# Layer-0 attention of a two-layer decoder trunk: the carry moved from DVE to ACT, third tiles for weights and probabilities, and a new instruction order

## The chip, the cores and the metric

The kernel runs on one core of a Trainium2 chip. The metric is the device time of one execution in microseconds (us), the median over runs. Work on the core goes to TensorE (PE, whose weight loads are listed apart as PEld), VectorE (DVE), ScalarE (ACT), GpSimd (POOL) and SyncE (SP), which here issues nearly all transfers.

## What is computed

A residual stream of 2048 tokens, with 16 meta tokens and padding ahead, goes through two layers and a final norm. The change lies in layer 0, an "even" layer with two attentions side by side, eight heads each: stick-breaking and a causal softmax (MLA).

```python
z = jnp.einsum('bthd,bshd->bhts', q, k) * scale          # stick-breaking
log_beta = jax.nn.log_sigmoid(z)
log_1m = jnp.where(mask, log_beta - z, 0.0)
suffix = lax.cumsum(log_1m, axis=3, reverse=True) - log_1m
a = jnp.where(mask, jnp.exp(log_beta + suffix), 0.0)
o_sb = jnp.einsum('bhts,bshd->bthd', a, v)
...
s = jnp.einsum('bthd,bshd->bhts', q, k) * scale          # causal softmax
p = jax.nn.softmax(jnp.where(mask, s, NEG), axis=-1)
o_mla = jnp.einsum('bhts,bshd->bthd', p, v)
...
h = h + jnp.concatenate([o_sb * silu(g_sb), o_mla * silu(g_mla)], -1) @ w_out
```

## The kernel before

Projections of layer 0 come first, then its attention (725 to 1624 us of the profiled execution), then its output projection and layer 1. Only the attention's order and three of its operations are touched.

The sequence is cut into 17 blocks of 122 keys. Heads are taken in 4 pairs (one head per half of the 128 output partitions), the queries in 5 groups g = 4, 3, 2, 1, 0 (four blocks of 122, so up to 488 columns; group 0 has one block). Within a pair and group, one step treats one key block of the stick-breaking part (from the diagonal back) and one of the softmax part (from the first key on). There are 17 + 13 + 9 + 5 + 1 = 45 steps a pair, 180 in all. Next to the diagonal a step is narrower: 366, 244 or 122 columns.

Each step, for both heads m = 0, 1 of the pair, consists of the operations below; the names are those of the planner, with the profile's line of before.

- stick-breaking: qks, two matmuls of scores into a PSUM tile zp (L1023, L1024); z, the mask at the diagonal on DVE (L1031); e, a softplus on ACT into sp (L1035); c, the carry: row 0 of the previous step's zp, scaled, goes to row 0 of this step's sp, on DVE (L1042); h, sp rounded to fp32r on DVE (L1050) or ACT (L1048); lo, sp minus h into l, on POOL or DVE (both L1055); tri, two matmuls of h and l with a triangular matrix, added to zp (L1060, L1061), which give the suffix sums and the next carry; a, a softplus on ACT of zp into the weights a (L1065); avs, the weights times the values into av (L1077).
- softmax: qkm, three matmuls of scores into ms (L1097 to L1099); p, on ACT into p, or acc in a group's first step (L1103); pm, the mask at the diagonal on DVE (L1109); acc, the sum of p over steps on POOL (L1115, L1117); avm, p times the values into mav (L1125).
- at a group's end: ogs and ogm (DVE, times the gates, L1087, L1131), dn, the denominators on PE (L1137), rd, their copy on ACT (L1142), rc, reciprocals on DVE (L1146), rm on POOL (L1150) and the stores.

The matmuls avs, avm and dn use 64 output columns, one head per half, so two of them stand side by side; the text calls them half-width, and a run of them between full-width matmuls a half-width run. Their inputs are f32 and show as two records for each matmul.

The order of each engine's instructions is fixed when the kernel is built. `attention_plan` lists the operations with planned costs and dependences; `list_schedule` then plays them through: an engine that is free takes, of the operations that are ready, the one of lowest rank (step number plus a constant `RANK` of its kind). `RINGS` says how many tiles there are of each kind, `MOVE` when h, lo or acc may go to another engine, `LAT` the planned delay between engines. The program emits the operations in that order, and semaphores make each wait for its inputs and tiles. An instruction that waits holds up whatever stands behind it on its engine.

Of the kernel before, what the change touches and what calls it, by code (L numbers as in the profile page):

```python
# [11 lines left out]
AF = mybir.ActivationFunctionType  # L12
ALU = mybir.AluOpType
# [113 lines left out]
def attention_plan():  # L127
# [34 lines left out]
    def gps(n):
        return n * 2.1 + 190

# [3 lines left out]
    for gi, (p, g) in enumerate(groups):  # L168
# [7 lines left out]
        tri, b_tri, acc, b_acc = ([None, None] for _ in range(4))  # L176
        prev = av = None
        for t in range(G.b1):
# [12 lines left out]
            for m in range(2):  # L191
                b_zp, b_a, b_sp, b_h, b_l = (buf(f"{x}{m}") for x in ("zp", "a", "sp", "h", "l"))
                qk_s = op("qks", s, m, "PE", pe(2, s.ns), [qk_s], [b_zp], late=late_s)
                o = qk_s
                if s.bs >= G.b0:
                    o = op("z", s, m, "DVE", 270, [o])
                o = op("e", s, m, "ACT", act(s.ns), [o], [b_sp])
                if prev:
                    o = op("c", s, m, "DVE", dve(prev.ns) + 60, [o, tri[m]], rel=[b_tri[m]])
                o = op("h", s, m, "DVE", dve(s.ns) + 200, [o], [b_h], alt=("ACT", act(s.ns)))  # L200
                o = op("lo", s, m, "Pool", gps(s.ns), [o], [b_l], [b_sp], alt=("DVE", 2.2 * dve(s.ns)))
                o = tri[m] = op("tri", s, m, "PE", pe(2, s.ns), [o], rel=[b_h, b_l])
                b_tri[m] = b_zp
                aa.append(op("a", s, m, "ACT", act(s.ns), [o], [b_a], [b_zp]))
                bz.append(b_a)
            pp, bp = [], []
            for m in range(2):
                b_ms, b_p = buf("ms"), buf(f"acc{m}" if s.first else f"p{m}")
                qk_m = op("qkm", s, m, "PE", pe(3, s.nm), [qk_m], [b_ms], late=late_m)
                x = op("p", s, m, "ACT", act(s.nm), [qk_m], [b_p], [b_ms])  # L210
                if s.bm >= G.b0:
                    x = op("pm", s, m, "DVE", 270, [x])
                pp.append(x)
                bp.append(b_p)
                if s.first:
                    acc[m], b_acc[m] = x, b_p
                else:
                    o = op("acc", s, m, "Pool", gps(s.nm), [x, acc[m]], rel=[b_p], alt=("DVE", 2.2 * dve(s.nm)))
                    acc[m] = o
                    if t == 1:  # L220
                        use(o, b_acc[m])
                        b_acc[m] = buf(f"acc{m}")
                        o.acq = [b_acc[m]]
            o = av = op("av", s, 0, "PE", pair(s.ns) + pair(s.nm) + 180, aa + pp + [av], [b_av, b_mav] if s.first else [],
                        bz + bp)
            if s.last:
# [13 lines left out]
    for o in ops:  # L240
        for d, w in o.deps:
# [9 lines left out]
HEAD = {("lo", "tri"): -200, ("a", "av"): -40, ("p", "av"): -40}
LAT = {("PE", "PE"): 0, ("PE", "ACT"): 200, ("PE", "DVE"): 200, ("PE", "Pool"): 250, ("ACT", "ACT"): 95,
       ("ACT", "PE"): 250, ("ACT", "DVE"): 200, ("ACT", "Pool"): 195, ("DVE", "DVE"): 60, ("DVE", "PE"): 320,
       ("DVE", "ACT"): 180, ("DVE", "Pool"): 230, ("Pool", "Pool"): 60, ("Pool", "PE"): 80, ("Pool", "DVE"): 80,
       ("Pool", "ACT"): 80}


def list_schedule(ops, rank=RANK, move=MOVE, rings=RINGS):
# [12 lines left out]
    busy = {e: 0 for e in engines}  # L271
    out, events, tick, now = [], [], 0, 0
    while len(out) < len(ops):
        again = True
        while again:
            again = False
            for e in engines:
                if busy[e] > now:
                    continue
                best = None  # L280
                for src in engines:
                    for o in ready[src]:
# [3 lines left out]
                        if any(len(held[b.ring]) >= rings[b.ring] and users[held[b.ring][-rings[b.ring]]] for b in o.acq):  # L286
                            continue
                        k = (pri[o][0] + (0 if own else rank["other"]), pri[o][1])
                        if best is None or k < best[0]:
                            best = (k, o, src)  # L290
                if best:
# [36 lines left out]
def build(tc, a, off, upto=99):  # L328
# [666 lines left out]
    with b2:  # L995
# [41 lines left out]
        def carry(s, m):  # L1037

            n, k = s.ns, s.prev.ns
            V.tensor_scalar(s.sp[m][0:1, n - k:n], s.prev.zp[m][0:1, :k], -1.0 / CW, None, op0=ALU.mult)  # L1042

# [19 lines left out]
        def aexp(s, m):  # L1063
            x = s.a[m] = work(f"a{m}", 2)
            S.activation(x[:BC, :s.ns], s.zp[m][:BC, :s.ns], AF.Softplus)  # L1065
# [35 lines left out]
        def pexp(s, m):  # L1101
            pt = s.pt[m] = work(f"acc{m}", 3) if s.first else work(f"p{m}", 2)
            S.activation(pt[:BK, :s.nm], s.ms[m][:BK, :s.nm], AF.Softplus, scale=MSC)  # L1103
            if s.first:
                s.G.acc[m] = pt
# [42 lines left out]
        def rmul(s, m):  # L1148
# [746 lines left out]
```

## Time and profile before

| | us |
|---|---|
| median of 3 runs | 2677.18 (2676.46 to 2677.35) |
| the profiled execution | 2672.08 |
| its span, first to last instruction | 2669.9 |
| outside the span | 2.2 |
| attention stage in it | 725 to 1624 |

| whole span | PE | PEld | DVE | ACT | POOL |
|---|---|---|---|---|---|
| busy us | 2570.5 | 1959.4 | 1587.2 | 1368.7 | 1123.5 |

The profile shows one execution. In a timeline row stand the start, the length, engine, line, operation, tiles, the number of instructions merged, and in brackets the idle time ahead of it with what the profile takes to have ended it. In a groups row stand the busy time, the mean length of one in ns and the idle time ahead. In a waits row stand the total in us, the times and the longest. A window row gives busy time and count for PE, PEld, DVE, ACT and POOL, then the granted PE clock (0.99 over the whole span), DMA share and GB/s. A wait is put down to the releaser that came last in the profile, which need not be the one that mattered.

### The profile page before, as it was taken

The page shows a single profiled execution, that of the slowest core. Times are in us where ns is not written, and L with a number is a line of the kernel's source. Part 1 is how long each engine was busy: PE and PEld are TensorE (multiplying, and loading weights), DVE is VectorE, ACT ScalarE, POOL GpSimd, SP SyncE. Part 2 cuts the span into 40 slices and gives each one's busy share as a digit, 9 for nine tenths or more (in the row PEclk, how much of TensorE's full clock was granted, in tenths as well). Part 3 has the DMA queues.
Part 4 walks back from the last instruction along what each step waited for, and adds up shares of the span by engine and source line. Part 5 has one row for each costly group of instructions (what it writes and reads, how often), then busy time and mean ns, then how long its engine had stood idle before and what let it go on. Part 6 is the DMA issues. An engine that isn't in the chain of part 4 may idle for free. (4 is left out here: it accounts for less than half of the span.)

```text
span 2669.9 us, 39152 instructions
## 1 busy us (share of the span) xinstructions
PE 2570.5 (96%) x13105; PEld 1959.4 (73%) x13105; DVE 1587.2 (59%) x3624; ACT 1368.7 (51%) x3143; POOL 1123.5 (42%) x925
## 2 busy tenths in 40 slices
PE   9999999999989999999999998999999899999998
PEld 7888889999855555555555556788999788777776
DVE  5366487777245665665575566334222567888884
ACT  6532121213255655565565553644222899986564
POOL 1012210010178878878878885300000123346551
PEclk9999999999999999999999999999999999999999
DMA  5376644342683352251230115534554345577652
GB/s 148 104 220 173 182 113 108 95 114 68 161 160 89 91 132 68 70 145 40 69 106 25 35 40 163 156 95 136 127 124 122 103 120 129 144 187 210 183 162 97
DMA packets 337860, 321.32 MB, mean 120 GB/s; under 512 B 143670, under 2 KB 319738, under 8 KB 337075
## 3 DMA queue, kind: packets, MB, share of 16 engines
q1 hardware_dynamic: 336939, 317.94, 44.6%
q8 instruction: 104, 1.70, 0.3%
q14 instruction: 97, 0.79, 0.1%
q10 hardware_dynamic: 720, 0.89, 0.1%
HBM read 198.28 MB, written 120.80 MB: 120 GB/s over the span
## 5 line engine op out<-in xcount | busy, mean ns | idle before, releaser
L1055 POOL TENSOR_TENSOR l<-sp,h 123x488 fp32r<-123x488 f32 (+2 forms) x334 | 364.3, 1095 | 109.4 <-DVE h L1050 72.0
L1597 POOL TENSOR_TENSOR s_sb<-s_sb,den 108x1008 f32<-108x1008 f32 (+1 forms) x76 | 147.4, 1940 | 548.5 <-DVE den L1596 451.9
L1117 POOL TENSOR_TENSOR acc<-acc,p 122x488 f32<-122x488 f32 (+3 forms) x288 | 329.1, 1160 | 32.0 <-ACT p L1103 17.5
L1042 DVE TENSOR_SCALAR sp<-zp 1x488 f32<-1x488 f32 (+3 forms) x320 | 183.4, 575 | 263.1 <-ACT p L1103 82.1
L406 PE MATMUL psd<-xh,wh 128*128 128x366 f32 (+1 forms) x760 | 273.8, 360 | 0.0
L408 PE MATMUL psd<-xh,wl 128*128 128x366 f32 (+1 forms) x760 | 267.3, 352 | 0.0
L407 PE MATMUL psd<-xl,wh 128*128 128x366 f32 (+1 forms) x760 | 267.2, 352 | 0.0
L1103 ACT ACTIVATE p<-ms 122x488 f32<-122x488 f32 (+3 forms) x320 | 151.9, 515 | 186.9 <-PE mav L1125 185.5
L1065 ACT ACTIVATE a<-zp 123x488 f32<-123x488 f32 (+2 forms) x360 | 175.6, 517 | 110.8 <-DVE sp L1042 80.6
L1035 ACT ACTIVATE sp<-zp 123x488 f32<-123x488 f32 (+2 forms) x360 | 180.4, 519 | 52.1 <-DVE zp L1031 26.9
L1050 DVE CAST h<-sp 123x488 fp32r<-123x488 f32 (+3 forms) x295 | 183.9, 623 | 13.2 <-ACT sp L1035 4.9
L1588 ACT ACTIVATE s_sb<-s_sb,nm 108x252 f32<-108x252 f32 (+1 forms) x304 | 149.2, 494 | 34.7 <-DVE nm L1579 34.7
L1023 PEld LDWEIGHTS zp<-q,kbig 128*123 128x123 f32 x320 | 58.8, 184 | 143.9 <-DVE h L1050 61.0
L1023 PE MATMUL zp<-q,kbig 128*123 128x488 f32 (+3 forms) x320 | 134.4, 424 | 22.9 <-ACT a L1065 19.1
L407 PEld LDWEIGHTS psd<-xl,wh 128*128 128x128 f32 x760 | 143.9, 189 | 15.8 <-issue 0.9
L406 PEld LDWEIGHTS psd<-xh,wh 128*128 128x128 f32 x760 | 143.7, 189 | 12.4 <-issue 0.7
L408 PEld LDWEIGHTS psd<-xh,wl 128*128 128x128 f32 x760 | 143.1, 188 | 10.8
L1077 PE MATMUL av<-a,vbig 123*64 123x488 f32 (+3 forms) x640 | 146.1, 535 | 2.3 <-DVE og L1087 2.3
L396 POOL TENSOR_TENSOR wl<-raw,wh 128x1024 fp32r<-128x1024 f32 x17 | 40.9, 2404 | 245.4 <-DVE wh L395 158.9
L1061 PE MATMUL zp<-l,tri_r 123*123 123x488 f32 (+2 forms) x360 | 132.2, 370 | 8.6 <-POOL l L1055 7.3
L1125 PE MATMUL mav<-p,mvbig 122*64 122x488 f32 (+3 forms) x640 | 139.0, 511 | 0.5 <-DMA mvbig<-d_mv 0.5
L1577 DVE CUSTOM_DVE_ANT_0 s_sb<-pss,bt,sinks 108x252 f32<-108x252 f32 (+1 forms) x304 | 127.3, 475 | 11.8 <-PE psg L1657 4.5
(516 smaller groups left out, 6850.0 us busy)
## 6 DMA issues: line engine op xcount, KB each, us to landing
kbig<-d_sk SPq DMA_DIRECT2D x32, 492.0 KB
q<-d_q SPq DMA_DIRECT2D x36, 432.0 KB
xt<-in_x SPq DMA_DIRECT2D x32, 448.0 KB
raw<-in_od_w_in SPq DMA_DIRECT2D x48, 256.0 KB
mq<-d_mq SPq DMA_DIRECT2D x32, 373.6 KB
raw<-in_ev_w_in SPq DMA_DIRECT2D x19, 512.0 KB
kkb<-d_kk SPq DMA_DIRECT2D x18, 472.0 KB
xt<-d_h SPq DMA_DIRECT2D x16, 512.0 KB
```

The lines of the kernel that those rows point to most:

```text
L406: T.matmul(o, wh[:, k, m0:m1], xh[:, k, c0:c1], start=(k == 0), stop=False)
L407: T.matmul(o, wh[:, k, m0:m1], xl[:, k, c0:c1], start=False, stop=False)
L408: T.matmul(o, wl[:, k, m0:m1], xh[:, k, c0:c1], start=False, stop=(k == k_n - 1))
L1023: T.matmul(zp[:BC, :s.ns], k[:, 2 * m, c], q, start=True, stop=False)
L1035: S.activation(sp[:BC, :s.ns], s.zp[m][:BC, :s.ns], AF.Softplus)
L1042: V.tensor_scalar(s.sp[m][0:1, n - k:n], s.prev.zp[m][0:1, :k], -1.0 / CW, None, op0=ALU.mult)
L1050: V.tensor_copy(h[:BC, :n], sp[:BC, :n])
L1055: on_(on).tensor_tensor(l[:BC, :n], s.sp[m][:BC, :n], f(s.h[m][:BC, :n]), op=ALU.subtract)
L1065: S.activation(x[:BC, :s.ns], s.zp[m][:BC, :s.ns], AF.Softplus)
L1103: S.activation(pt[:BK, :s.nm], s.ms[m][:BK, :s.nm], AF.Softplus, scale=MSC)
L1117: eng.tensor_tensor(g.acc[m][:BK, s.jm:g.n], g.acc[m][:BK, s.jm:g.n], s.pt[m][:BK, :n], op=ALU.add)
L1588: S.activation(s_sb[:nq, hh, :ww], s_sb[:nq, hh, :ww], AF.Exp, bias=nm[:nq, hh:hh + 1], scale=SLOPES[h], accum_out=den[:nq, hh:hh + 1])
```

## The change

The carry c becomes an ACT instruction (an activation that copies, with a scale) instead of DVE's. The rings of a and p get three tiles instead of two. In the planner, av is split into avs and avm, which can be ordered apart; its costs and delays have new numbers; a price `TURN` is put on PE going to half width, with two ranks that steer it (`few`: wait while fewer than two half-width operations are ready; `stay`: remain at half width once there). `RANK` and `MOVE` are new numbers. Everything outside the attention keeps its order; line numbers are 13 higher from qks to a and 9 higher from avs on.

```diff
     def pe(passes, n):
-        return passes * max(n / 2.24 + 6, 107)
+        return passes * max(n / 2.244 + 5, 107)
     def pair(n):
-        return 4 * (n / 2.38 + 2) + 140
+        return n / 0.6
     def dve(n):
-        return n / 0.96 + 69
+        return n / 0.96 + 75
     def act(n):
-        return n / 1.2 + 85
+        return n / 1.2 + 70
+    def two(n):
+        return n * 2.45 + 110
     def gps(n):
-        return n * 2.1 + 190
+        return n * 2.1 + 215
...
-                    o = op("c", s, m, "DVE", dve(prev.ns) + 60, [o, tri[m]], rel=[b_tri[m]])
-                o = op("h", s, m, "DVE", dve(s.ns) + 200, [o], [b_h], alt=("ACT", act(s.ns)))
-                o = op("lo", s, m, "Pool", gps(s.ns), [o], [b_l], [b_sp], alt=("DVE", 2.2 * dve(s.ns)))
+                    o = op("c", s, m, "ACT", act(prev.ns), [o, tri[m]], rel=[b_tri[m]])
+                o = op("h", s, m, "DVE", s.ns * 1.3 + 150, [o], [b_h], alt=("ACT", act(s.ns)))
+                o = op("lo", s, m, "Pool", gps(s.ns), [o], [b_l], [b_sp], alt=("DVE", two(s.ns)))
...
-            o = av = op("av", s, 0, "PE", pair(s.ns) + pair(s.nm) + 180, aa + pp + [av], [b_av, b_mav] if s.first else [],
-                        bz + bp)
+            av = op("avs", s, 0, "PE", pair(s.ns), aa + [av], [b_av] if s.first else [], bz)
+            mav = op("avm", s, 0, "PE", pair(s.nm), pp + [mav], [b_mav] if s.first else [], bp)
...
-RINGS = dict(... a0=2, a1=2, ... p0=2, p1=2, ...)
+RINGS = dict(... a0=3, a1=3, ... p0=3, p1=3, ...)
-MOVE = dict(lo=849, acc=1901, h=104)
+MOVE = dict(lo=829, acc=3122, h=0)
+HALF_WIDTH = ("avs", "avm", "dn")
+TURN = 342
...
+                if e == "PE":
+                    few = rank["few"] * (sum(o.kind in HALF_WIDTH and rt[o] <= now for o in ready[e]) < 2)
...
+                        if o.kind in HALF_WIDTH:
+                            k = (k[0] - rank["stay"] if half else k[0] + few, k[1])
...
+                    o.took = o.cost if src == e else o.alt[1]
+                    if e == "PE":
+                        o.took += TURN * (o.kind in HALF_WIDTH and not half)
+                        half = o.kind in HALF_WIDTH
...
-            V.tensor_scalar(s.sp[m][0:1, n - k:n], s.prev.zp[m][0:1, :k], -1.0 / CW, None, op0=ALU.mult)
+            S.activation(s.sp[m][0:1, n - k:n], s.prev.zp[m][0:1, :k], AF.Copy, scale=-1.0 / CW)
...
-        def values(s, _):
-            avs(s)
-            avm(s)
```

What moves is shown at one place, the full-width step 100 of the 180 (its score matmuls to its value passes: about 1220 to 1241 us in the profile of before). A row is a line, the operation, the tile written and the tiles read, and the size; digits behind a name are the head (sp0, sp1) and a tile's number.

ACT in before, from e of head 0 of step 100 on:

```order
L1035 ACTIVATE sp0_11826<-zp0_11816 123x488
L1103 ACTIVATE p0_11842<-ms_11808 122x488
L1103 ACTIVATE p1_11846<-ms_11822 122x488
L1065 ACTIVATE a0_11852<-zp0_11770 123x488
L1065 ACTIVATE a1_11858<-zp1_11793 123x488
L1035 ACTIVATE sp1_11866<-zp1_11839 123x488
```

ACT in after, from the same e on (L1048 is e, L1055 the carry, L1061 h, L1078 a, L1112 p):

```order
L1048 ACTIVATE sp0_11856<-zp0_11842 123x488
L1048 ACTIVATE sp1_11863<-zp1_11849 123x488
L1055 ACTIVATE sp0_11856<-zp0_11802 1x488
L1055 ACTIVATE sp1_11863<-zp1_11808 1x488
L1061 ACTIVATE h1_11878<-sp1_11863 123x488
L1078 ACTIVATE a0_11886<-zp0_11802 123x488
L1078 ACTIVATE a1_11888<-zp1_11808 123x488
L1112 ACTIVATE p0_11892<-ms_11858 122x488
L1112 ACTIVATE p1_11897<-ms_11868 122x488
```

A step has six ACT instructions before, and eight or nine after: both carries, and in every second step one h, stand between e and a.

DVE in before, steps 100 and 101:

```order
L1042 TENSOR_SCALAR sp0_11826<-zp0_11770 1x488
L1050 CAST h0_11860<-sp0_11826 123x488
L1042 TENSOR_SCALAR sp1_11866<-zp1_11793 1x488
L1050 CAST h1_11881<-sp1_11866 123x488
L1042 TENSOR_SCALAR sp0_11872<-zp0_11816 1x488
L1050 CAST h0_11906<-sp0_11872 123x488
L1042 TENSOR_SCALAR sp1_11912<-zp1_11839 1x488
L1050 CAST h1_11927<-sp1_11912 123x488
```

DVE in after, from step 100 on (L1063 is h, L1068 lo):

```order
L1063 CAST h0_11873<-sp0_11856 123x488
L1068 TENSOR_TENSOR l1_11882<-sp1_11863,h1_11878 123x488
L1063 CAST h0_11918<-sp0_11903 123x488
L1063 CAST h1_11926<-sp1_11907 123x488
L1063 CAST h0_11965<-sp0_11948 123x488
L1068 TENSOR_TENSOR l1_11974<-sp1_11955,h1_11970 123x488
```

The carries are gone from DVE; one h of four has gone to ACT, and one lo of four has come from POOL. Over the whole stage, lo on POOL goes from 334 to 253 and on DVE from 26 to 107; h on DVE goes from 295 to 263 and on ACT from 65 to 97. acc stays on POOL (320).

PE in before, around the half-width run that holds the value passes of step 98:

```order
L1099 MATMUL ms_11854<-mq_11253,mkbig4_10118 122x488
L1023 MATMUL zp0_11862<-q_11237,kbig0_10783 123x488
L1024 MATMUL zp0_11862<-q_11237,kbig0_10783 123x488
L1097 MATMUL ms_11868<-mq_11253,mkbig4_10118 122x488
L1098 MATMUL ms_11868<-mq_11253,mkbig4_10118 122x488
L1099 MATMUL ms_11868<-mq_11253,mkbig4_10118 122x488
L1077 MATMUL av_11527<-a0_11806,vbig0_10785 64x488
L1077 MATMUL av_11527<-a1_11812,vbig0_10785 64x488
L1125 MATMUL mav_11530<-p0_11796,mvbig0_10786 64x488
L1125 MATMUL mav_11530<-p1_11800,mvbig0_10786 64x488
L1023 MATMUL zp1_11885<-q_11237,kbig0_10783 123x488
```

PE in after, at the run that holds avs of step 96, avm of 98 and avs of 97 (L1086 is avs, L1134 avm, L1036 qks):

```order
L1106 MATMUL ms_11868<-mq_11189,mkbig4_10074 122x488
L1107 MATMUL ms_11868<-mq_11189,mkbig4_10074 122x488
L1108 MATMUL ms_11868<-mq_11189,mkbig4_10074 122x488
L1086 MATMUL av_11570<-a0_11732,vbig4_10075 64x488
L1086 MATMUL av_11570<-a1_11747,vbig4_10075 64x488
L1134 MATMUL mav_11425<-p0_11760,mvbig0_10742 64x488
L1134 MATMUL mav_11425<-p1_11764,mvbig0_10742 64x488
L1086 MATMUL av_11570<-a0_11794,vbig4_10075 64x488
L1086 MATMUL av_11570<-a1_11796,vbig4_10075 64x488
L1036 MATMUL zp0_11894<-q_11283,kbig0_10739 123x488
L1037 MATMUL zp0_11894<-q_11283,kbig0_10739 123x488
L1036 MATMUL zp1_11900<-q_11283,kbig0_10739 123x488
```

Before, each step's two value passes form one run, between the score matmuls of head 0 and head 1 of one step. After, two runs stand in two steps: one with three passes, of steps 96 to 98, as here, and one with avm alone; the score matmuls of both heads come together. Over the stage there are 187 half-width runs before and 165 after.

More of the change, by code (lines that the diff above doesn't have):

```diff
@@ L176, in attention_plan @@
         tri, b_tri, acc, b_acc = ([None, None] for _ in range(4))
-        prev = av = None
+        prev = av = mav = None
         for t in range(G.b1):
@@ L211, in attention_plan @@
                 if s.bm >= G.b0:
-                    x = op("pm", s, m, "DVE", 270, [x])
+                    x = op("pm", s, m, "DVE", 300, [x])
                 pp.append(x)
@@ L217, in attention_plan @@
                 else:
-                    o = op("acc", s, m, "Pool", gps(s.nm), [x, acc[m]], rel=[b_p], alt=("DVE", 2.2 * dve(s.nm)))
+                    o = op("acc", s, m, "Pool", gps(s.nm), [x, acc[m]], rel=[b_p], alt=("DVE", two(s.nm)))
                     acc[m] = o
@@ L246 @@
 DMA_NS = 6000
-RINGS = dict(zp0=2, zp1=2, a0=2, a1=2, sp0=2, sp1=2, h0=2, h1=2, l0=2, l1=2, av=1, mav=1, ms=2,
-             p0=2, p1=2, acc0=3, acc1=3, og=2, rd=1)
-RANK = dict(qks=-15.42, z=10.15, e=21.37, rc=-14.75, c=-16.52, h=27.44, lo=-11.85, tri=-8.67, a=-7.29, av=26.38, ogs=21.25, qkm=-2.11, p=-8.52, pm=-4.52, acc=-36.25, ogm=5.1, dn=1.09, rd=-4.23, rm=0.64, head=0.54, other=2.43)
-MOVE = dict(lo=849, acc=1901, h=104)
[L251 to L255, printed above, removed]
+RINGS = dict(zp0=2, zp1=2, a0=3, a1=3, sp0=2, sp1=2, h0=2, h1=2, l0=2, l1=2, av=1, mav=1, ms=2,
+             p0=3, p1=3, acc0=3, acc1=3, og=2, rd=1)
+RANK = dict(qks=-48.53, z=-16.4, e=36.5, rc=-42.98, c=-9.66, h=11.42, lo=-30.91, tri=-5.03, a=4.01, avs=5.07, avm=3.11, ogs=23.02, qkm=-2.2, p=-10.76, pm=2.07, acc=-41.78, ogm=12.82, dn=-0.45, rd=8.86, rm=-7.51, head=0.23, other=11.93, few=12.47, stay=8.39)
+MOVE = dict(lo=829, acc=3122, h=0)
+HEAD = {("lo", "tri"): -200, ("a", "avs"): -40, ("p", "avm"): -40}
+HALF_WIDTH = ("avs", "avm", "dn")
+TURN = 342
+LAT = {("PE", "PE"): 0, ("PE", "ACT"): 200, ("PE", "DVE"): 250, ("PE", "Pool"): 250, ("ACT", "ACT"): 45,
+       ("ACT", "PE"): 200, ("ACT", "DVE"): 80, ("ACT", "Pool"): 155, ("DVE", "DVE"): 60, ("DVE", "PE"): 160,
+       ("DVE", "ACT"): 50, ("DVE", "Pool"): 145, ("Pool", "Pool"): 0, ("Pool", "PE"): 30, ("Pool", "DVE"): 0,
+       ("Pool", "ACT"): 0}
 def list_schedule(ops, rank=RANK, move=MOVE, rings=RINGS):
@@ L271, in list_schedule @@
     busy = {e: 0 for e in engines}
-    out, events, tick, now = [], [], 0, 0
+    out, events, tick, now, half = [], [], 0, 0, False
     while len(out) < len(ops):
@@ L296, in list_schedule @@
                     o.on, o.start = e, now
-                    busy[e] = now + (o.cost if src == e else o.alt[1])
+                    o.took = o.cost if src == e else o.alt[1]
+                    if e == "PE":
+                        o.took += TURN * (o.kind in HALF_WIDTH and not half)
+                        half = o.kind in HALF_WIDTH
+                    busy[e] = now + o.took
                     tick += 1
@@ L1063, in aexp, with avs @@
         def aexp(s, m):
-            x = s.a[m] = work(f"a{m}", 2)
+            x = s.a[m] = work(f"a{m}", RINGS[f"a{m}"])
             S.activation(x[:BC, :s.ns], s.zp[m][:BC, :s.ns], AF.Softplus)
-        def values(s, _):
-            avs(s)
-            avm(s)
-        def avs(s):
+        def avs(s, _):
             if s.first:
@@ L1101, in pexp @@
         def pexp(s, m):
-            pt = s.pt[m] = work(f"acc{m}", 3) if s.first else work(f"p{m}", 2)
+            pt = s.pt[m] = work(f"acc{m}", 3) if s.first else work(f"p{m}", RINGS[f"p{m}"])
             S.activation(pt[:BK, :s.nm], s.ms[m][:BK, :s.nm], AF.Softplus, scale=MSC)
@@ L1117, in accum, with avm @@
                 eng.tensor_tensor(g.acc[m][:BK, s.jm:g.n], g.acc[m][:BK, s.jm:g.n], s.pt[m][:BK, :n], op=ALU.add)
-        def avm(s):
+        def avm(s, _):
             if s.first:
@@ L1151, in rmul @@
             put(g).dma_start(d_og[g.g][:, 4 + g.p], g.og[:, :n])
-        RUN = dict(qks=qks, z=zmask, e=soft, c=carry, h=high, lo=low, tri=tri, a=aexp, av=values, ogs=ogs,
+        RUN = dict(qks=qks, z=zmask, e=soft, c=carry, h=high, lo=low, tri=tri, a=aexp, avs=avs, avm=avm, ogs=ogs,
                    qkm=qkm, p=pexp, pm=pmask, acc=accum, ogm=ogm, dn=den, rd=rden, rc=recip, rm=rmul)
```

9 lines of the change are left out of this document (5 added, 4 removed).

## The prediction

> **What bounds the kernel now.** I read the windows first, to see which engine is full in the attention stage, then the waits there, then the timeline of one steady step on PE, and only then the groups that price the moved work. The first rows are the stage cut into its first 25 us, its long middle and its last 24 us.
>
> ```profile
> 725.00:750.00 25.00, 20.09 (x85) 13.51 (x85) 11.56 (x24) 12.74 (x29) 15.79 (x15) 0.86 1.06 231
> 750.00:1600.00 850.00, 814.08 (x3819) 473.20 (x3819) 519.05 (x952) 504.92 (x1096) 716.26 (x643) 1.00 0.32 80
> 1600.00:1624.00 24.00, 21.24 (x126) 12.68 (x124) 19.07 (x38) 14.62 (x39) 14.76 (x16) 0.97 0.29 99
> ```
>
> The columns are PE, PEld, DVE, ACT, POOL. In the middle PE is busy 814 of 850 us, POOL 716 (84%), DVE 519, ACT 505 (59%). PE's busy time contains overlapped ends, so the starts of one step tell more. This is PE over one step of full width (488 columns):
>
> ```profile
> 1222.41 1.04 PE L1077 MATMUL av<-a,vbig 123*64 123x488 f32 x4
> 1223.28 0.99 PE L1125 MATMUL mav<-p,mvbig 122*64 122x488 f32 x4
> 1224.20 0.49 PE L1023 MATMUL zp<-q,kbig 128*123 128x488 f32 x1
> 1224.52 0.39 PE L1024 MATMUL zp<-q,kbig 128*123 128x488 f32 x1
> ...
> 1226.08 0.38 PE L1099 MATMUL ms<-mq,mkbig 96*122 96x488 f32 x1
> 1226.78 0.49 PE L1023 MATMUL zp<-q,kbig 128*123 128x488 f32 x1 [0.32 <-ACT a L1065]
> 1227.11 0.38 PE L1024 MATMUL zp<-q,kbig 128*123 128x488 f32 x1
> ...
> 1227.77 0.38 PE L1099 MATMUL ms<-mq,mkbig 96*122 96x488 f32 x1
> 1228.08 1.04 PE L1077 MATMUL av<-a,vbig 123*64 123x488 f32 x4
> ```
>
> The step takes 5.67 us (1222.41 to 1228.08). From 1224.52 to 1226.08 seven matmuls start, one each 0.223 us: that is PE's price of a full-width matmul. After 1226.08 the next starts 0.70 later instead of 0.22, and its partner 0.33 later. So about 0.5 us is a wait for a; all in all 0.57 of the 5.67 will turn out not to be work. What a is waiting for stands on the other engines at the same time:
>
> ```profile
> 1225.46 0.65 DVE L1042 TENSOR_SCALAR sp<-zp 1x488 f32<-1x488 f32 x1 [1.98 <-ACT p L1103]
> ...
> 1228.39 0.75 DVE L1050 CAST h<-sp 123x488 fp32r<-123x488 f32 x1
> ...
> 1224.36 1.05 ACT L1103 ACTIVATE p<-ms 122x488 f32<-122x488 f32 x2 [1.85 <-PE mav L1125]
> 1226.15 1.05 ACT L1065 ACTIVATE a<-zp 123x488 f32<-123x488 f32 x2 [0.74 <-DVE sp L1042]
> ...
> 1225.08 2.60 POOL L1117 TENSOR_TENSOR acc<-acc,p 122x488 f32<-122x488 f32 x2 [0.20 <-ACT p L1103]
> 1227.65 1.22 POOL L1055 TENSOR_TENSOR l<-sp,h 123x488 fp32r<-123x488 f32 x1
> 1229.31 1.23 POOL L1055 TENSOR_TENSOR l<-sp,h 123x488 fp32r<-123x488 f32 x1 [0.45 <-DVE h L1050]
> ```
>
> The carry on DVE runs 1225.46 to 1226.11; a on ACT starts at 1226.15, right behind it, since both read the same zp; PE's next score matmul starts when a is done. That is the loop that sets 5.67. POOL is next: 2.60 + 1.22 + 1.23 of work, with gaps of 0.45 and 0.20. The 0.45 is its wait for the second h, which ended at 1229.14, 0.27 after the POOL instruction of 1227.65 ended (1228.87). Summed over the stage the same waits are:
>
> ```profile
> ACT p L1103 <- PE mav L1125: 185.5, 133, 1.9
> ...
> ACT a L1065 <- DVE sp L1042: 80.6, 103, 2.0
> ...
> POOL l L1055 <- DVE h L1050: 72.0, 132, 4.1
> ...
> PEld zp L1023 <- ACT a L1065: 54.1, 93, 1.0
> ...
> PE zp L1023 <- DMA kbig<-d_sk: 3.5, 1, 3.5
> ```
>
> **PE's work, and so its idle time.** Four rows give the widths of one of seven full-width matmul lines (the others have the same 360 instructions), and two pairs of starts the price of narrow ones; the last four rows show half-width passes inside one run.
>
> ```profile
> L1060 PE MATMUL zp<-h,tri_r 123*123 123x488 f32 x256 | 100.7, 393 | 0.0
> ...
> L1060 PE MATMUL zp<-h,tri_r 123*123 123x366 f32 x32 | 11.4, 356 | 0.0
> ...
> L1060 PE MATMUL zp<-h,tri_r 123*123 123x244 f32 x32 | 10.4, 324 | 0.0
> ...
> L1060 PE MATMUL zp<-h,tri_r 123*123 123x122 f32 x40 | 9.2, 247 | 0.0
> ```
>
> ```profile
> 1248.49 0.34 PE L1098 MATMUL ms<-mq,mkbig 96*122 96x366 f32 x1
> 1248.66 0.33 PE L1099 MATMUL ms<-mq,mkbig 96*122 96x366 f32 x1
> ...
> 1265.65 0.27 PE L1060 MATMUL zp<-h,tri_r 123*123 123x122 f32 x1
> 1265.76 0.27 PE L1061 MATMUL zp<-l,tri_r 123*123 123x122 f32 x1
> ```
>
> ```profile
> 1276.68 0.99 PE L1125 MATMUL mav<-acc,mvsmall 122*64 122x488 f32 x4
> 1277.50 0.58 PE L1077 MATMUL av<-a,vbig 123*64 123x244 f32 x4
> 1277.91 0.99 PE L1125 MATMUL mav<-p,mvbig 122*64 122x488 f32 x4
> 1278.83 0.48 PE L1023 MATMUL zp<-q,kbig 128*123 128x488 f32 x1
> ```
>
> Full width: 256 x 0.223 + 32 x 0.17 + 32 x 0.115 + 40 x 0.107 = 70.5 us a line, 493 for seven. A half-width pass costs 0.82 at 488 columns and 0.41 at 244, in proportion to its columns. The 360 value passes (half of 360 each kind, 180 steps) are 2 x (128 x 0.82 + 16 x 0.61 + 16 x 0.41 + 20 x 0.20) = 250, and 20 denominators add 14. A turn to half width and back costs the differences around a run: 0.31 - 0.22 ahead (1227.77 to 1228.08), 0.87 - 0.82 in the first pass, 0.92 - 0.82 behind the last, 0.32 - 0.22 in the first full-width matmul: 0.34. The order of before has 187 such runs: 64. Sum 821 of 899 us. Of the 78 idle, filling and draining take at least 7.7 (PE is busy 20.09 of the first 25 and 21.24 of the last 24); since busy time holds overlaps, I take 12. 66 are waits that an order can remove.
>
> **The change, part by part.**
>
> Turns: the order of after has 165 half-width runs instead of 187: 22 x 0.34 = 7.5 us of PE, on the path. The planner's repriced costs act through the order alone. The transfers are the same ones, issued behind the same steps; the longest wait of PE for a load is one of 3.5 us (last row of the waits above), so I price them at nothing.
>
> Carry to ACT. The groups that price the moved work are these:
>
> ```profile
> L1042 DVE TENSOR_SCALAR sp<-zp 1x488 f32<-1x488 f32 (+3 forms) x320 | 183.4, 575 | 263.1 <-ACT p L1103 82.1 <-ACT sp L1035 76.1 <-POOL acc L1117 36.1
> ...
> L1142 ACT ACTIVATE rd<-dn 128x488 f32<-128x488 f32 (+1 forms) x20 | 10.5, 526 | 5.8 <-POOL og L1150 4.2 <-PE dn L1137 1.6
> ...
> L1055 POOL TENSOR_TENSOR l<-sp,h 123x488 fp32r<-123x488 f32 (+2 forms) x334 | 364.3, 1095 | 109.4 <-DVE h L1050 72.0 <-ACT h L1048 27.1 <-ACT a L1065 9.4
> ```
>
> DVE loses 183 us. No row has ACT reading one partition. From below: two p take 1.05 together, so the second costs 0.47 when nothing waits between them; from above, DVE's 0.65 for one at 488. Nearest is the copy out of PSUM of the same length (L1142, 0.526 mean), which is ACT as well; I take 0.5, so 320 x 0.5 = 160 us, with 138 to 184 as ends. 32 more h move to ACT by the new order: 16 us. On the path this costs nothing as long as PE's part of a step covers ACT's eight or nine instructions (some 4.3 us at 0.5); without that cover a carry costs its 0.5 in full. ACT goes from 505 to about 681 of the middle, 80 to 85% of a shorter stage. The carry now stands in ACT's queue, and behind a carry that waits for tri stand a, p and the next e; who waits for those is PE's tri and score matmuls.
>
> Low parts to DVE: 81 of the 334 leave POOL (253 stay). POOL loses 81 x 1.095 = 89 us at most. The port sets the other end: the h above ended 0.27 after POOL's instruction, so DVE work on SBUF waits for POOL and POOL for it. If a moved low part holds POOL for a whole unhindered DVE pass (0.575, L1042's mean as the nearest DVE pass), POOL wins 81 x 0.52 = 42. I take 65, between, because the h rows show POOL held for only part of a pass. POOL then stands at about 650 of a shorter middle.
>
> The Trainium skill, "SBUF — State Buffer", section "SBUF: two separate sides", says that a DVE instruction with two SBUF inputs and a GpSimd instruction exclude each other for the whole instruction. By it the 42 would hold, and it speaks against this part of the change; the cast that ended 0.27 behind POOL's end agrees with the waiting, but no row here shows the whole length of the hold. As an estimate by this rule, the sum ends at the port rival's 2656 below instead of 2630.
>
> A third tile for a and p removes the wait of p for mav (185.5 us), which is ACT's and costs PE nothing by itself; it lets avs stand two to three steps behind its a, which is what joins value passes of two steps into one run.
>
> **The steady step after.** Two steps form one cycle in the new order: 28 full-width matmuls (6.24), four half-width passes (3.28), two turns (0.68): 10.2, or 5.10 a step instead of 5.67. Does anything else hold it? Count from the first score matmul. tri ends near 1.4 and 2.5, the three-pass half-width run stands from 3.3 to 5.7. ACT: carries at 1.9 and 2.9, h to 4.0, then a waits for the a tile that the first pass of that run frees (4.4), a and p are done at 6.0; the next score matmuls (5.7) need only the first a, read by 5.0. POOL: two acc from 1.9 to 4.5, one low part to 6.2, needed by tri at 6.7. In the second half the carries come at 7.5 and 8.0, h waits for POOL's second acc (8.8), the low parts end at 10.4 and 11.9, and the later tri starts at 12.3. PE is the bound, with 0.3 to 0.7 us to spare. I leave 0.1 a step as lost: 0.47 gained, in 56 steps (so many of the 179 intervals between the first value matmuls of two steps are 5.60 to 5.75; the one shown is of these): 26 us.
>
> The other 124 steps, narrow ones at the diagonal, hold 66 - 56 x 0.57 = 34 us of idle. Their order changes too, but in no pattern that I can walk through; I take a third of it away (13), with 0 and 34 as ends.
>
> Sum: 7.5 + 26 + 13 = 46.5. The profiled execution took 2672.08 (span 2669.9), so 2625.6; the median of the runs is 5.1 higher, and I forecast 2630 for it. 0.2% (5 us) is about what a measurement can tell from no change.
>
> **The rivals.**
>
> The port eats the relief: h and low on DVE wait behind POOL and hold it, by the lower price of 42 us or less, and the spare of 0.3 us at the later tri is gone. For it: 72.0 us of POOL waits for h already. Against it: POOL was not what PE waited for in the steady step. Half the steady gain and nothing at the diagonal are left: 7.5 + 13, so 2656.
>
> The waits go nearly everywhere: 7.5 + 60 or more, 2605 and less. For it: every engine but PE ends under 85%. Against: the narrow steps chain z, e, carry, h, low, tri one after the other.
>
> ACT's queue becomes the bound, and it is slower: in the narrow steps a carry that waits for tri holds up the e and p behind it, and DVE's idle time does not help. ACT's 15 to 20% of slack speaks against, its fixed order for it. It decides where each of the 124 narrow steps loses 0.38 us more than now (46.5 / 124); at 0.5 us it is 2692.
>
> The order only trades one wait for another, and PE's idle stays at 66: the turns alone, within 0.2% or just beyond, 2670 to 2677.
>
> **How the numbers follow.** Forecast (2605 to 2645) 0.60; port 0.17; nearly all waits gone 0.09; no effect 0.06; ACT slower 0.08. Faster: 0.60 + 0.17 + 0.09 and a share of the fourth, 0.87; same 0.05; slower 0.08. The range takes in the forecast, most of the port rival and a part of the low one: 2600 to 2664.
>
> **What would show it.** Right: full-width steps near 5.1 to 5.2 us; no wait of a for a carry; p no longer waits for mav; POOL under 80%; ACT's carry about 0.5 us; fewer but longer half-width runs; everything before 725 us and behind the stage unchanged. Wrong: low parts on DVE of 1.3 us and more with POOL's next instruction as long, PE's tri waiting for low (port), or e and p waiting behind a carry while PE waits for a or zp (ACT).

## The result, and the profile after

| | before | after |
|---|---|---|
| median, us | 2676.82 | 2612.68 |
| profiled execution, us | 2672.08 | 2614.04 |
| its span, us | 2669.9 | 2612.3 |

The ratio after to before is 0.9763 (95% interval 0.9746 to 0.9780): 64 us by the medians, 58 by the profiled executions. Medians here and below leave out two executions that took far longer than all others: 4465.7 us of the kernel with reordered loads, and 5381.4 us of before on the same chip. The forecast was 2630 (2600 to 2664), so the direction and the range held, and the gain was larger than the 47 that the sum gave.

The stage now ends at 1567 instead of 1623 us. The row gives the first and the last start of av's matmuls on one kind of value tile, the last of the stage among them; before, the last such start is at 1623.0:

```profile
L1086 PE MATMUL av<-a,vsmall x80: 267/572/911, 832.3 to 1566.7; 123*64 123x488 f32 x64, 123*64 123x122 f32 x16
```

The windows of after, columns as before (PE, PEld, DVE, ACT, POOL): the first 25 us and the long middle of the stage.

```profile
725.00:750.00 25.00, 17.33 (x65) 11.01 (x64) 10.78 (x19) 14.56 (x37) 13.61 (x13) 0.86 1.02 222
750.00:1540.00 790.00, 783.46 (x3818) 486.15 (x3819) 463.27 (x693) 626.85 (x1431) 628.83 (x560) 0.99 0.34 87
```

PE is busy 783 of 790 us. ACT went from 59% to 79% and POOL from 84% to 80%. The timeline of PE over one cycle of two full-width steps shows what became of the step:

```profile
1201.55 1.04 PE L1086 MATMUL av<-a,vbig 123*64 123x488 f32 x4
1202.42 0.99 PE L1134 MATMUL mav<-p,mvbig 122*64 122x488 f32 x4
1203.24 0.99 PE L1086 MATMUL av<-a,vbig 123*64 123x488 f32 x4
1204.16 0.49 PE L1036 MATMUL zp<-q,kbig 128*123 128x488 f32 x1
1204.48 0.38 PE L1037 MATMUL zp<-q,kbig 128*123 128x488 f32 x1
...
1207.15 0.39 PE L1108 MATMUL ms<-mq,mkbig 96*122 96x488 f32 x1
1207.46 1.04 PE L1134 MATMUL mav<-p,mvbig 122*64 122x488 f32 x4
1208.43 0.48 PE L1036 MATMUL zp<-q,kbig 128*123 128x488 f32 x1
...
1211.75 1.04 PE L1086 MATMUL av<-a,vbig 123*64 123x488 f32 x4
```

From 1201.55 to 1211.75 are 10.20 us for two steps, 5.10 each: exactly PE's price of the work, with no wait left in it. Between 1204.48 and 1207.15 twelve matmuls start at 0.22 each. These are waits of PE's matmuls in the stage (waits view, PE only):

```profile
PE zp L1036 <- DMA kbig<-d_sk: 5.0, 1, 5.0
PE ms L1106 <- DMA mkbig<-d_kr: 4.1, 1, 4.1
...
PE zp L1074 <- DVE l L1068: 1.4, 7, 0.2
```

No PE row names ACT's a any more, where before 19.1 us stood; the longest that are left are two loads at the start of the stage. The list of the weight loads, which the prediction also read, still names a, with more than the 54.1 us of before:

```profile
PEld zp L1036 <- ACT a L1078: 77.6, 109, 1.2
```

That row is no loss by itself. The run at 1207.46 above is followed by such a gap of the weight loads (0.77 us), yet the next score matmul starts 0.97 behind its first pass, which is the price of one pass and its turn (0.82 + 0.05 + 0.10). So the distances of starts decide, not this list. ACT's waits and the price of the carry:

```profile
ACT sp L1055 <- PE zp L1074: 42.1, 54, 5.4
...
ACT p L1112 <- PE mav L1134: 24.0, 44, 2.2
```

```profile
L1055 ACT ACTIVATE sp<-zp 1x488 f32<-1x488 f32 (+3 forms) x320 | 154.0, 495 | 44.9 <-PE zp L1074 42.1
```

The wait of p for mav fell from 185.5 to 24.0, and a carry costs ACT 0.495 us. The wait of a for the carry is gone from ACT's list, but it had to be: both are now instructions of one engine, and what can be seen instead is the carry's own wait for tri, 42.1. The stage's surroundings did not change: from the first instruction to the first score matmul pass 722 us before and 724 after, from the last value matmul to the end 1046 and 1046.

### The profile page after: what moved, and what is told of

Read it like the earlier page. It is cut to its first block, busy times and chain, and to the rows that moved or that the text cites. A ratio compares the mean times of both kernels' runs of the same rounds, so it can differ in the third digit from the quotient of the medians.

```text
span 2612.3 us, 38920 instructions
## 1 busy us (share of the span) xinstructions
PE 2543.0 (97%) x13105; PEld 1976.7 (76%) x13105; DVE 1532.4 (59%) x3353; ACT 1493.4 (57%) x3495; POOL 1038.1 (40%) x844
## 5 line engine op out<-in xcount | busy, mean ns | idle before, releaser
L1063 DVE CAST h<-sp 123x488 fp32r<-123x488 f32 (+3 forms) x263 | 179.1, 686 | 268.6 <-ACT sp L1055 245.6
L1068 POOL TENSOR_TENSOR l<-sp,h 123x488 fp32r<-123x488 f32 (+3 forms) x253 | 295.0, 1173 | 102.5 <-DVE h L1063 84.1
L1126 POOL TENSOR_TENSOR acc<-acc,p 122x488 f32<-122x488 f32 (+3 forms) x288 | 310.6, 1098 | 40.6 <-DVE p L1118 25.2
L1048 ACT ACTIVATE sp<-zp 123x488 f32<-123x488 f32 (+2 forms) x360 | 172.7, 516 | 58.2 <-DVE zp L1044 27.6
L1078 ACT ACTIVATE a<-zp 123x488 f32<-123x488 f32 (+2 forms) x360 | 167.4, 503 | 42.2 <-PE zp L1074 25.5
L1055 ACT ACTIVATE sp<-zp 1x488 f32<-1x488 f32 (+3 forms) x320 | 154.0, 495 | 44.9 <-PE zp L1074 42.1
L1112 ACT ACTIVATE p<-ms 122x488 f32<-122x488 f32 (+3 forms) x320 | 150.5, 513 | 25.4 <-PE mav L1134 24.0
L1036 PEld LDWEIGHTS zp<-q,kbig 128*123 128x123 f32 x320 | 58.9, 184 | 112.4 <-ACT a L1078 61.8
L1134 PE MATMUL mav<-p,mvbig 122*64 122x488 f32 (+3 forms) x640 | 143.9, 528 | 0.0
L1086 PE MATMUL av<-a,vbig 123*64 123x488 f32 (+3 forms) x640 | 142.7, 524 | 0.0
L1068 DVE TENSOR_TENSOR l<-sp,h 123x488 fp32r<-123x488 f32 (+3 forms) x107 | 129.1, 1212 | 16.6 <-ACT h L1061 13.1
L1036 PE MATMUL zp<-q,kbig 128*123 128x488 f32 (+3 forms) x320 | 127.4, 401 | 7.8 <-DMA kbig<-d_sk 5.0
```

The source lines that it names most:

```text
L1036: T.matmul(zp[:BC, :s.ns], k[:, 2 * m, c], q, start=True, stop=False)
L1048: S.activation(sp[:BC, :s.ns], s.zp[m][:BC, :s.ns], AF.Softplus)
L1055: S.activation(s.sp[m][0:1, n - k:n], s.prev.zp[m][0:1, :k], AF.Copy, scale=-1.0 / CW)
L1063: V.tensor_copy(h[:BC, :n], sp[:BC, :n])
L1068: on_(on).tensor_tensor(l[:BC, :n], s.sp[m][:BC, :n], f(s.h[m][:BC, :n]), op=ALU.subtract)
L1126: eng.tensor_tensor(g.acc[m][:BK, s.jm:g.n], g.acc[m][:BK, s.jm:g.n], s.pt[m][:BK, :n], op=ALU.add)
```

## The experiments

Each kernel is compared with before on the same chip; "x us" are medians. The gain of the whole change is 64.

**The carry back on DVE, in the order of after.**

```diff
-            S.activation(s.sp[m][0:1, n - k:n], s.prev.zp[m][0:1, :k], AF.Copy, scale=-1.0 / CW)
+            V.tensor_scalar(s.sp[m][0:1, n - k:n], s.prev.zp[m][0:1, :k], -1.0 / CW, None, op0=ALU.mult)
```

> The order of after, each carry at its place but executed by DVE again. Theory (the order gained, by keeping a and the next score matmuls away from the carry, and PE is the bound with 0.3 to 0.7 us to spare a step): a carry takes 0.65 instead of 0.5 and a must still follow it, which the spare absorbs in full-width steps; 2612 to 2628, full-width steps stay near 5.1 to 5.2. Rival (the engine of the carry gave most of the gain): over 2640, with waits of a for the carry of 60 us or more on PE's path.

2633.6 us, ratio 0.9839 (0.9824 to 0.9854): 21 slower than after, 6 above my range. PE's timeline (rows of avs) shows the full-width cycle all the same:

```profile
1199.65 1.04 PE L1086 MATMUL av<-a,vbig 123*64 123x488 f32 x4
...
1209.83 1.04 PE L1086 MATMUL av<-a,vbig 123*64 123x488 f32 x4
```

10.18 us for two steps, against 10.20 in after. So in steady full-width steps the carry's engine is worth next to nothing once the order stands. Most of the loss lies in and around the narrow steps, where the spare that I had counted for wide ones does not exist: the stage is 16 us longer than in after's profiled execution, and only 3 of them stand in full-width stretches (the table at the end of this section says how that is counted). The wait that came back on ACT is this one, in the waits view:

```profile
ACT a L1078 <- DVE sp L1055: 59.7, 91, 1.9
```

On PE itself stand 6.5 us of score matmuls that wait for the carry and 4.6 of tri that waits for low; after has no row of the first kind and 0.2 of the second.

**The carry on ACT, in the order of before** (the same two lines the other way round, nothing else).

> The order of before, with nothing changed but that ACT executes the carry at its place. Theory (the order gained): the loop tri, carry, a, next score matmul stays, and is shorter only by what ACT's carry is shorter than DVE's, 0.65 - 0.5 = 0.15 to 0.2 a step; 2655 to 2675. Rival (the engine of the carry gave most of the gain): 2640 or less. Rival (ACT's in-order queue costs more than it saves while the order is old): over 2682.

2657.2, ratio 0.9930 (0.9915 to 0.9945): 19 faster than before, in the range of the first theory. The step is 5.40 (1211.36 to 1216.76), which is 0.27 shorter and more than the 0.15 to 0.2 that the theory had. What holds this step at 5.40 is no longer a, as these rows of PE and one of POOL show:

```profile
1211.36 1.04 PE L1077 MATMUL av<-a,vbig 123*64 123x488 f32 x4
...
1214.12 0.38 PE L1060 MATMUL zp<-h,tri_r 123*123 123x488 f32 x1
1214.51 0.48 PE L1061 MATMUL zp<-l,tri_r 123*123 123x488 f32 x1
...
1216.76 1.04 PE L1077 MATMUL av<-a,vbig 123*64 123x488 f32 x4
```

```profile
1213.21 1.24 POOL L1055 TENSOR_TENSOR l<-sp,h 123x488 fp32r<-123x488 f32 x1 [0.41 <-PE mav L1125]
```

The late matmul is the second of tri (0.39 behind the first instead of 0.22), right behind the end of POOL's low part (1214.45), and the score matmul of head 1, at 1215.50, is on time. Over the full-width stretches of this kernel tri comes late 38 times and that score matmul 37 times; in before it was the score matmul alone, 56 times.

**Three tiles, in the order of before.**

```diff
-            x = s.a[m] = work(f"a{m}", 2)
+            x = s.a[m] = work(f"a{m}", 3)
-            pt = s.pt[m] = work(f"acc{m}", 3) if s.first else work(f"p{m}", 2)
+            pt = s.pt[m] = work(f"acc{m}", 3) if s.first else work(f"p{m}", 3)
```

> The order of before, with nothing changed but that a and p have three tiles. Theory: the 185 us that p waits for mav are ACT's and not on the path; 2670 to 2680, the wait gone and PE's times the same. Rival (the third tile is worth something by itself, since p earlier makes acc and POOL earlier): 2660 or less.

2668.7, ratio 0.9967 (0.9955 to 0.9980): 7 faster, 1.3 below the range. In the waits view ACT's largest wait changes its name:

```profile
ACT a L1065 <- DVE sp L1042: 212.7, 109, 2.7
```

p no longer waits for mav, and ACT waits for the carry instead (212.7 against 80.6 before). 185 us of wait taken away were worth 7.

**All low parts on POOL, in the order of after.**

```diff
-            on_(on).tensor_tensor(l[:BC, :n], s.sp[m][:BC, :n], f(s.h[m][:BC, :n]), op=ALU.subtract)
+            G.tensor_tensor(l[:BC, :n], s.sp[m][:BC, :n], f(s.h[m][:BC, :n]), op=ALU.subtract)
```

> The order of after, with the 107 low parts that stand on DVE executed by POOL at their place. Theory (POOL would be the next bound, at 5.1 of work plus the waits at the port against PE's 5.10 a step): full-width steps go to 5.4 to 5.7, 2630 to 2655. Rival (POOL was never on the path, and the relief is worth nothing): 2608 to 2620.

2647.5, ratio 0.9893 (0.9878 to 0.9908): 35 slower than after. The size was expected, the place was not. The full-width cycle stays at 10.20 (rows of avs on PE):

```profile
1216.96 1.04 PE L1086 MATMUL av<-a,vbig 123*64 123x488 f32 x4
...
1227.16 1.04 PE L1086 MATMUL av<-a,vbig 123*64 123x488 f32 x4
```

POOL's work fits into 5.10 there. The loss is in and around the narrow steps again (30 of the 33 us by which the stage is longer, by that table), and PE's wait for the low part grew, from 0.2 us in after:

```profile
PE zp L1074 <- POOL l L1068: 24.8, 53, 0.9
```

The groups of POOL, first in after, then here, give what a low part on DVE relieves:

```profile
L1126 POOL TENSOR_TENSOR acc<-acc,p 122x488 f32<-122x488 f32 (+3 forms) x288 | 310.6, 1098 | 40.6 <-DVE p L1118 25.2 <-ACT p L1112 15.2 <-POOL acc L1126 0.2
L1068 POOL TENSOR_TENSOR l<-sp,h 123x488 fp32r<-123x488 f32 (+3 forms) x253 | 295.0, 1173 | 102.5 <-DVE h L1063 84.1 <-ACT h L1061 11.5 <-PE zp L1037 4.3
```

```profile
L1068 POOL TENSOR_TENSOR l<-sp,h 123x488 fp32r<-123x488 f32 (+2 forms) x360 | 389.7, 1094 | 79.9 <-DVE h L1063 66.5 <-ACT h L1061 6.9 <-PE zp L1037 3.2
L1126 POOL TENSOR_TENSOR acc<-acc,p 122x488 f32<-122x488 f32 (+3 forms) x288 | 308.4, 1089 | 11.7 <-DVE p L1118 8.1 <-ACT p L1112 3.6
```

107 low parts fewer on POOL make 698.1 - 605.6 = 92.5 us less work there, 0.86 each. The moved ones are narrower than the mean: 55, 24, 8 and 20 of 488, 366, 244 and 122 columns, which by the means of these widths here (1.257, 0.987, 0.707 and 0.446) would be 107.4 us, 1.00 each. So 0.14 each is taken back as longer instructions of POOL.

How the two engines meet shows at two places of after, first with DVE ahead, then with POOL ahead:

```profile
1202.29 0.67 DVE L1068 TENSOR_TENSOR l<-sp,h 123x488 fp32r<-123x488 f32 x1
1202.41 1.62 POOL L1068 TENSOR_TENSOR l<-sp,h 123x488 fp32r<-123x488 f32 x1 [0.35 <-DVE h L1063]
...
1212.44 1.23 POOL L1068 TENSOR_TENSOR l<-sp,h 123x488 fp32r<-123x488 f32 x1 [0.35 <-DVE h L1063]
1212.48 1.71 DVE L1068 TENSOR_TENSOR l<-sp,h 123x488 fp32r<-123x488 f32 x1
```

Whoever comes second is the longer one: POOL by 0.39, and DVE until 0.52 behind the end of POOL's instruction. Of the 55 full-width low parts on DVE 44 start while a POOL instruction runs, and end 0.52 behind it in the median; 10 start just ahead of one, take 0.65, and POOL's takes 1.59.

**The turns unpriced.**

```diff
-RANK = dict(... few=12.47, stay=8.39)
-TURN = 342
+RANK = dict(... few=0.0, stay=0.0)
+TURN = 0
```

> After, with the planner's price of a turn to half width and the two ranks that hold runs together at zero: 280 half-width runs instead of 165, all else the same. Theory (a turn costs PE 0.34 us, and PE has next to no idle time left to hide it): 115 x 0.34 = 39 us more than after, 2640 to 2665. Rival (turns stand beside waits and are mostly hidden): 2612 to 2630.

2656.8, ratio 0.9925 (0.9909 to 0.9941), the span 2652.4: 40.1 more than after's for 115 runs more, 0.35 each, against 0.34 in the sum. The instructions stand in another order as well; the table at the end of this section shows that the rest of the stage stayed as it was.

**Two tiles, replanned.**

```diff
-RINGS = dict(... a0=3, a1=3, ... p0=3, p1=3, ...)
+RINGS = dict(... a0=2, a1=2, ... p0=2, p1=2, ...)
```

> After, with two tiles for a and p, in the plan and in the kernel: the same ranks now give 219 half-width runs, since avs can stand less far behind its a. Theory (what the third tiles buy is longer runs, 54 x 0.34 = 18 us, and some freedom beside them): 2630 to 2655. Rival (the third tiles are not needed): 2608 to 2620.

2632.2, ratio 0.9830 (0.9813 to 0.9847), span 2631.9: 19.6 more than after for 54 runs more, 0.36 each. The third tiles, with this order, are worth what their longer half-width runs save. These ranks were not chosen for two tiles, so others could do better.

**The order of before with both edits** (the carry on ACT and three tiles).

> The order of before, with the carry executed by ACT and three tiles for a and p: the whole change but for the order. Theory (the order holds what is left): the two add up, -19 and -7, 2645 to 2658, full-width steps at 5.40 as with the carry alone. Rival (carry and tiles help each other, and the order is a small part): 2630 or less.

2649.3, ratio 0.9896 (0.9881 to 0.9911): 28.6 faster than before, against 19 + 7 = 26 for the two alone. What is left to after, 36.6 us, is the order, together with the engines that it gives to h and lo; 22 turns (7.5) are part of it. A step of it on PE, ACT and POOL (timeline) shows what held it at 5.38 (1214.75 to 1220.13):

```profile
...
1217.29 0.39 PE L1061 MATMUL zp<-l,tri_r 123*123 123x488 f32 x1
1217.51 0.38 PE L1060 MATMUL zp<-h,tri_r 123*123 123x488 f32 x1
1217.81 0.48 PE L1061 MATMUL zp<-l,tri_r 123*123 123x488 f32 x1
...
1218.57 0.38 PE L1099 MATMUL ms<-mq,mkbig 96*122 96x488 f32 x1
1218.85 0.48 PE L1023 MATMUL zp<-q,kbig 128*123 128x488 f32 x1
```

```profile
1217.77 0.57 ACT L1042 ACTIVATE sp<-zp 1x488 f32<-1x488 f32 x1 [1.59 <-PE zp L1061]
1218.24 1.01 ACT L1065 ACTIVATE a<-zp 123x488 f32<-123x488 f32 x2
```

```profile
1216.52 1.24 POOL L1055 TENSOR_TENSOR l<-sp,h 123x488 fp32r<-123x488 f32 x1 [0.42 <-DVE h L1050]
```

Two small waits of PE stand there. The second matmul of tri starts at 1217.81, 0.05 behind POOL's low part (1216.52 + 1.24), and the score matmul at 1218.85, when the first a (1218.24 + about 0.58) is through (0.28 behind the last, instead of 0.22).

**The same, with h of head 1 on ACT in full-width steps**, which ends POOL's wait for that h.

```diff
-            if on == "ACT":
+            if on == "ACT" or (m == 1 and n == 488):
                 S.activation(h[:BC, :n], sp[:BC, :n], AF.Copy)
```

> As the run of before's order with carry on ACT and three tiles (full-width steps 5.40, where POOL has 2.60 + 1.22 + 1.24 of work and 0.42 of waiting for the second h, which DVE can only do at the port once POOL's instruction ends), but the h of head 1 in full-width steps is done by ACT. Theory (POOL and the port set 5.40): POOL's 0.42 goes, full-width steps at 5.10 to 5.2, 2630 to 2642. Rival (something else on PE or ACT sets 5.40): 5.35 to 5.45, 2645 to 2655.

2635.3, ratio 0.9845 (0.9829 to 0.9860), in the range; but the step is 5.39 (1203.29 to 1208.68), so the theory fell for the step it was made for:

```profile
1203.29 1.04 PE L1077 MATMUL av<-a,vbig 123*64 123x488 f32 x4
...
1205.88 0.38 PE L1061 MATMUL zp<-l,tri_r 123*123 123x488 f32 x1
1206.10 0.38 PE L1060 MATMUL zp<-h,tri_r 123*123 123x488 f32 x1
1206.32 0.39 PE L1061 MATMUL zp<-l,tri_r 123*123 123x488 f32 x1
...
1206.98 0.38 PE L1099 MATMUL ms<-mq,mkbig 96*122 96x488 f32 x1
1207.38 0.48 PE L1023 MATMUL zp<-q,kbig 128*123 128x488 f32 x1
...
1208.68 1.04 PE L1077 MATMUL av<-a,vbig 123*64 123x488 f32 x4
```

The wait for low is gone (1206.10 to 1206.32), and the wait for a took its place: 1207.38 instead of 1207.20. From the second matmul of head 0's tri to that score matmul pass 1.50 us (1205.88 to 1207.38; 1.56 in the run above), and the order puts six distances of 0.22 there, 1.3 us. So two chains end almost together in that order, POOL's low part and tri, carry, a, and taking one away leaves the other. The run is 14 us faster all the same. Laid beside the run above, whose matmuls stand in the same order, its profiled execution gains 1 us in full-width stretches and 10 elsewhere in the stage, around the narrow steps; 4 more lie outside the stage. Which wait it is there stays open.

**Fewer turns**: other numbers in RANK and MOVE, 154 runs.

> After, with other ranks that give 154 half-width runs instead of 165. Theory (PE is the bound and each run less is 0.34 us): 3.8 us less than after, 2605 to 2612. Rival (the narrow steps lose by the other order what the turns give): 2613 to 2625.

2617.8, ratio 0.9778 (0.9763 to 0.9792), span 2616.9: 4.6 more than after, not 3.8 less. The result is in the rival's range. Two rows of PEld and PE that grew (2.1 us in after for the first, none for the second):

```profile
PEld zp L1074 <- POOL l L1068: 8.2, 22, 0.6
...
PE zp L1036 <- ACT sp L1055: 2.6, 4, 0.7
```

**The first loads in another order**, and after once more beside it.

```diff
-        load_mv(0, 1)
         load_k(0, 3, mla=False)
-        load_k(0, 2)
+        load_mv(0, 1)
+        load_k(0, 2, sb=False)
+        load_k(0, 2, mla=False)
```

> After, with the stage's first loads in another order: the scores' keys of group 3 ahead of the values of group 1, and the softmax keys of group 2 ahead of its stick-breaking keys. PE waits 5.0 and 4.1 us for these two loads in after. Theory: each lands 1 to 3 us earlier, 2607 to 2611 beside 2613. Rival (the transfer engines are full there, and another load is late instead): 2612 to 2616.

> After once more, unchanged, beside the run with reordered loads: 2610 to 2616.

2608.0, ratio 0.9742 (0.9729 to 0.9756), beside 2614.1, ratio 0.9762 (0.9749 to 0.9775), for after. The loads that PE waits for at the start of the stage are now these; after beside it waited 4.2 us for the scores' keys and 3.2 for the softmax keys:

```profile
PE zp L1036 <- DMA kbig<-d_sk: 3.5, 1, 3.5
PE mav L1134 <- DMA mvbig<-d_mv: 1.3, 1, 1.3
```

The wait for the softmax keys is gone, that for the scores' keys is shorter, and the values of group 1 are late instead, by less. It is the fastest kernel of all, and its four executions (2605.6 to 2610.5) lie below all five of after (2610.7 to 2616.8), but the two intervals overlap, so the 5 to 6 us are likely rather than shown.

**What is left between PE's starts.** The traces allow one more reading of all these kernels. Price each of PE's matmuls in the stage as the prediction does (the distance to the next start where nothing waits: 0.22, 0.17, 0.11 and 0.107 at full width, 0.82, 0.61, 0.41 and 0.21 for a half-width pass), which makes 755 us in every kernel, and add 0.34 for each half-width run. The rest of the stage, from its first matmul's start to its last one's, is waiting. It is split here into full-width stretches, where the twelve matmuls on each side all have 488 columns, and all others. These are sums over the profiled executions; the two of after differ by 3, and a value just under zero comes from rounded prices. Within one order the stretches are the same matmuls; before's are 301 us long and after's 179, so across the orders the split is only a rough one.

| us | stage | turns | rest | in full-width stretches | elsewhere |
|---|---|---|---|---|---|
| before | 901 | 64 | 83 | 33 | 50 |
| three tiles, order of before | 898 | 64 | 80 | 32 | 48 |
| carry on ACT, order of before | 883 | 64 | 64 | 18 | 46 |
| both edits, order of before | 875 | 64 | 57 | 17 | 40 |
| the same, h of head 1 on ACT | 864 | 64 | 46 | 16 | 31 |
| after | 843 | 56 | 32 | -1 | 33 |
| after once more | 840 | 56 | 29 | -1 | 30 |
| after, first loads in another order | 836 | 56 | 25 | -1 | 26 |
| carry back on DVE | 859 | 56 | 48 | 2 | 46 |
| low parts on POOL | 876 | 56 | 65 | 2 | 63 |
| turns unpriced | 882 | 95 | 32 | 4 | 29 |
| two tiles, replanned | 861 | 75 | 32 | 2 | 31 |
| fewer turns | 846 | 52 | 39 | 1 | 38 |

With the turns unpriced, and with two tiles, the rest is the 32 of after: what they lose is, as far as these sums go, turns alone. In after 9 of the 32 are the waits for the two loads, and part is the granted clock: it is 0.51 to 0.52 in 741 to 748, 751 to 758 and 1154 to 1157.4 us of after, and in before 0.53 in 738 to 745. In the stretch at 1154 a half-width pass takes 1.68 us instead of 0.87.

## Why the prediction was right, and where its sizes were off

- **The bound.** Right: PE's work with its turns is the floor of the stage, and the loop tri, carry, a, score matmul held the step above it. The carry on ACT alone took the step from 5.67 to 5.40. There a second chain, through POOL's low part, ends nearly together with the first, which the prediction had not seen behind it; with POOL relieved the step stayed at 5.39. The new order took it to 5.10.
- **Turns.** Right. 7.5 us in the sum at 0.34 each; measured 0.35 and 0.36 on 115 and 54 runs, with the rest of the stage unchanged.
- **Steady steps.** Too small. I left 0.1 us a step as lost and counted 26 us; the step came out at 5.10, which makes 56 x 0.57 = 32; the table has 33 and -1. The walk through the cycle was right, and the reserve on top of it had no row behind it.
- **The other steps.** Too small. I counted 13 of 34 us (called a third, which would be 11), with no row for the share. The spans differ by 57.6; without 7.5 and 32, some 18 are left for the 124 narrow steps and the rest, and the table has 50 and 33. Two of the experiments say what they need: the carry back on DVE costs 21 us and the low parts back on POOL 35, most of it outside full-width stretches. The diagonal needs the relief of both engines, while I had argued with wide steps. How the 18 divide between the causes stays open.
- **Loads.** Priced at nothing, and not nothing: PE waits 5.0 and 4.1 us for the two first loads in after (3.5 and 0.7 for the same loads in before), and putting these loads in another order gave some 5 us, likely rather than shown.
- **The median.** The profiled execution of before was 4.7 below the median, that of after 1.4 above its own. So 6 of the 64 us between the medians are the spread of single executions, and no term of the sum.
- **Carry on ACT.** 0.5 taken, 0.495 measured. Off the path in full-width steps as said, but not at the diagonal.
- **Low parts.** 65 of 81 x 1.095 taken, 0.80 each; 0.86 measured, of 1.00 by width. The Trainium skill, "SBUF — State Buffer", section "SBUF: two separate sides", has the loser of the port blocked for the whole instruction, which I had turned into 0.52 of relief. The traces agree with the blocking, but not with that use of it: 44 of the 55 full-width low parts on DVE are themselves the loser, so most of the waiting is theirs. Only 0.14 each shows as longer POOL instructions; waiting that falls into POOL's idle time would not show there.
- **The rivals.** The port did not eat the relief, though half of its sign came: full-width low parts on DVE take 1.35 us in the mean, above the 1.3 that was to tell, in after's groups by form.

```profile
L1068 DVE TENSOR_TENSOR l<-sp,h 123x488 fp32r<-123x488 f32 x55 | 74.5, 1354 | 16.0 <-ACT h L1061 12.9
```

The other half, tri waiting for low, stayed at 1.4 us on DVE's and 0.2 on POOL's. ACT's queue did not become the bound (79% busy, and its longest wait in sum is 42.1 us, for tri). The result lies nearer to the rival of nearly no waits than to the forecast. That rival's 2605 was worked out from the profiled execution (2672 - 67.5), while the others start from the median; from there it is 2610, inside the band that the forecast claimed. So the mechanism and the direction were right, and the range held, but the sum had 47 where 58 to 64 came.

## What to carry to other kernels

When an engine is busy 96% of a stage, price its instructions by the distance of their starts and look for the loop that makes the rest; here a wait of 80 us on ACT was part of that loop, while the larger one of 185 us was worth 7. An edit that shortens the loop (the carry on ACT, 19 us) can run into the next chain at once, and was worth less than an order that takes both off the path (37 us more); buffers pay by what the order does with them. Try such a walk on the narrow steps too: what has spare in a wide step may have none at the edges.

## What the runs showed of the hardware

Going from 128 output columns to 64 and back cost PE 0.34 to 0.36 us in these kernels: 115 and 54 such runs more left the rest of the stage as it was. An activation on one partition of 488 columns takes about as long as on 123 (0.555 against 0.578 for the softplus e, in after's groups by form); over all widths the carry took 0.495 on ACT, where DVE took 0.575. A low part on DVE and an instruction of POOL did not run side by side: the second of the two ended 0.52 us behind POOL's end, or POOL's took 1.59 us instead of 1.23.
